# Retention q and k projections of an encoder trunk as four blocks of seven half-size products, with another order of the attention section and a planner that counts latencies between engines

## The chip, the cores and the metric

The kernel runs on one core of one Trainium2 chip. The metric is the device time of one execution in microseconds (us); a run of the comparison takes several executions, and their median is used. The profile comes from one further execution, recorded instruction by instruction. Engine names in it: PE is the matrix engine (PEld its weight loads), DVE the vector engine, ACT the scalar engine, POOL the GpSimd engine, SP the engine that issues plain DMAs.

## The reference, cut to what matters

Two encoder layers on 512 tokens of width 1024, in float32. Each layer has one wide input projection whose columns are split into the parts below; the change touches how `q_r` and `k_r` (512 columns each, four heads of 128) are computed.

```python
IN_SIZES = (NA_W, NA_W, NA_W, RET_QK_W, RET_QK_W, RET_V_W, RET_V_W, D_MODEL, D_MODEL)
...
    for i in range(DEPTH):
        proj = x @ w_in[i]
        q_na, k_na, v_na, q_r, k_r, v_r, g_r, gate_a, gate_b = jnp.split(proj, IN_SPLITS, axis=-1)
        ya = neighbourhood_attention(...)
        yb = bidirectional_retention(q_r.reshape(B, T, RET_HEADS, RET_QK_DIM),
                                     k_r.reshape(B, T, RET_HEADS, RET_QK_DIM),
                                     v_r, g_r, ret_decay_f[i], ret_decay_b[i])
        merged = jax.nn.sigmoid(gate_a) * (ya @ w_branch_a[i]) + jax.nn.sigmoid(gate_b) * (yb @ w_branch_b[i])
        y = merged @ w_out[i]
        x = layer_norm(DEEPNORM_ALPHA * x + y, ln1_g[i], ln1_b[i])
        ffn = conv_glu_ffn(x, w_up[i], conv_w[i], conv_b[i], w_down[i])
        ple = jax.nn.sigmoid(x @ w_ple_gate[i]) * (p[i] @ w_ple_proj[i])
        x = layer_norm(DEEPNORM_ALPHA * x + ffn + ple, ln2_g[i], ln2_b[i])
    return x
```

Retention rotates q and k (rotary embedding), forms decayed scores within a chunk and a decayed state across chunks, normalises each head and gates it.

## The kernel before

**Precision.** Every float32 operand of a product is split into a high and a low part (`split`: ACT casts `hi`, DVE subtracts to get `lo`), and `mm3` makes each product from three matmuls: hi by hi, hi by lo, lo by hi. A 512 KB chunk of weights thus costs one cast on ACT and one subtraction on DVE before PE can use it. Chunks marked "sent" (here those with numbers 20 to 23, among others) get `lo` from a second DMA that adds the weights onto the negated `hi`, so they cost no DVE instruction.

**Two ways to make a projection.** A plain tile (`gemm_t`) is 128 output columns by all 512 tokens: 8 pieces of the depth times 3 matmuls, 24 matmuls of 512 moving columns, into a PSUM bank named `gt`. A block is a two-by-two arrangement of tiles computed by seven half-size products (Strassen's scheme in Winograd's form), named a, c, t1, t2, d, t3 and t4; each is 24 matmuls of 256 moving columns (`product_t`, L1717) into banks named `u`, `v` and `w`. A block reads four weight chunks; the weights of t1, t2, t3 and t4 are sums of chunks, made in place by four accumulating DMAs from POOL. The sums of activations (`Sx`, tiles `sh` and `sl`) exist anyway. For a block of q and k tiles, `qk_block` (L1759) gathers the seven results into two SBUF tiles `uh` through `halves` (L1744), four times by a copy on ACT and three times by an addition on DVE, and hands the halves to the functions that follow a projection. In the kernel before, the three gate blocks 2, 3, 4 and the two blocks 5, 6 of attention q and k run this way; blocks 7 and 8 (retention q and k) are written in the code but not in the order, and retention q and k are the eight plain tiles `q0` to `q3` and `k0` to `k3` of a layer.

**The attention section** of a layer is the walk through the tuple `FILL` (L46): an entry such as `2t1` is product t1 of block 2, `R0` the next of four steps of retention head 0 (scores and the transposed k; state; output and group norm; transposition of the result into `ybt`), `N0` the next of three steps of attention head 0 (scores and softmax; transposition `pt`; output `na`), `vn` a piece of the attention values, `bb0` a tile of the retention branch's output projection, `xn` the load of the residual. After it come the merge (`mt`), the output projection, the first layer norm (`proj_ln`, `done1`, which transposes the normalised rows back with PE), and the gated MLP.

**The planner.** From the attention section to the last but one down-projection of a layer, the order of every engine's instructions is worked out when the program is built, by a list scheduler (`_order`, L466): it keeps a modelled time, a cost for each instruction (`_costs`), due times, counts of free buffers, and starts on each engine the first instruction in order of due time whose inputs are ready. PE keeps the written order, but in the attention section it may take any of the next `FILL_WIN` = 10 products. The due times are shaken by random numbers from the seeds in `SET`, one entry per layer, and `_best` repeats the pass up to 12 times with raised priority for what PE waited on. On the chip the engines run these fixed orders and wait for each other through semaphores.

A reader will meet these names: `lo`, `hi` the two parts of a weight chunk (`rawa`, `rawt`, `raw` the chunk itself), `t` and `kf` the rotated q and k, `qk` their split, `kz` the decayed k, `ta` and `a` the decayed scores, `yb` the normalised head, `qn`, `kn`, `kl` the attention q and k, `S` the attention scores, `xn` the residual rows, `x1t` the normalised activations.

```python
            def qk_block(b, kind):
                ps, first = bank_of(b, kind)
                product_t(kind, ps, first)
                st = keep.setdefault(b, {})
                i = halves(kind, st, ps)
                if i is not None:
                    h = st[i]
                    m = 2 * (b - 5 if b < 7 else b - 7) + 1 - i
                    for f, g in enumerate((na_q, na_k) if b < 7 else (q_head, k_head)):
                        g(m, h[:, f])
```

Of the kernel before, what the change touches and what calls it, by code (L numbers as in the profile page):

```python
# [42 lines left out]

FILL_WIN = 10
FILL_AT = (36, 40, 56, 24, 28, 8, 20)
FILL = (tuple('2a 3a 2c 3c q0 2t1 3t1 k0 2t2 3t2 2d 3d 4a 2t3 3t3 4c 2t4 4t1 k1 3t4 4t2 R0 4d q1 R0 4t3 R0 4t4 5a R0 R1 5c 5t1 k2 R1 q2 R1 5t2 5d R2 q3 R1 6a 6c R2 k3 R2 5t3 5t4 R3 6t1 6t2 R2 6d 6t3 R3 N0 N1 6t4 R3 vn N0 N1 vn R3 N2 vn N3 vn N0 N1 N2 bb0 N3 N4 bb1 N5 N6 bb2 N2 N4 N7 bb4 N3 N5 N6 bb5 N7 bb6 N4 bb7 N5 N6 xn N7 bb3'.split()),) * 2  # L46
ORD = ('vector', 'scalar', 'tensor', 'gpsimd', 'sync')
RESIDENT = {(l, c) for l in range(DEPTH) for c in range(68, 72)}

# [16 lines left out]

DOWN = ("a", "c", "t1", "t2", "d", "t3", "t4")
CAP = {"unit.u": 30, "xt.xt": 1, "raw.raw": 3, "wsplit.hi": 3, "wsplit.lo": 3, "tmp.t": 6, "bias.tb": 2, "bias.cw": 2, "bias.B": 2, "psum.b": 8}
COST = {"issue": 1.0, "send": 0.4, "load": 1.45, "add": 3.0, "land": 4.2}
EARLY = {"w": 14, "g": 13, "s": 15, "c": 13, "d": 13, "t3": 14, "a": 28, "t1": 38, "t2": 30, "t4": 18}  # L70
AHEAD, OVERLAP = 14, 0.08
_SET = dict(soon=5, hold=6, reserve=10, load=16, work=25, scale=1.0, spare=2, near=10, seed=0, shake=0.0)
SET = {1: dict(soon=3, hold=6, reserve=4, load=14, work=25, scale=1.0, spare=1, near=10, seed=651, shake=1), 2: dict(soon=3, hold=10, reserve=8, load=16, work=30, scale=1.0, spare=0, near=14, seed=903, shake=2)}
ROUNDS = 12


# [242 lines left out]
def _costs(o):  # L319
# [3 lines left out]
    if "dma" in o.name:  # L323
        o.dur = COST["issue"] if o.eng == "gpsimd" else COST["send"]
        ref = next((x for x in o.outs + o.ins if isinstance(x, Ref) and x.parts is not None), None)
        o.dma = (COST["add"] if o.k.get("accum_op") is not None else COST["load"]) * _size(ref) / 1024
        o.land = COST["land"]
    elif o.eng == "vector":
# [59 lines left out]
def _dues(jobs):  # L388

    soon = lambda j: SET[j.plan]["soon"] if j.plan else 5  # L390

# [74 lines left out]
def _order(jobs):  # L466
# [18 lines left out]
    for e in ENGINES:  # L485
# [6 lines left out]
        if e != "tensor":  # L492
            for p, s in segs:
                if p:
                    seed, amount = SET[p]["seed"], SET[p]["shake"]
                    rnd = random.Random(seed * 7 + len(e))
# [4 lines left out]
    free_at = {e: 0.0 for e in ENGINES}  # L501
    heap, t, pipe, order, lag, table = [0.0], 0.0, 0.0, [], 0.0, 0
    back, count, total, lost = [], 0, len(jobs), 0.0
    held = {}
    while count < total:
# [5 lines left out]
        for e in ENGINES:  # L511
# [66 lines left out]
            j = best  # L578
# [5 lines left out]
                x.pop(j, None)  # L584
            j.start = t
            j.done = t + dur
            free_at[e] = j.done - (OVERLAP if e in ("vector", "scalar") else 0.0)
            if j.dma:
                pipe = max(pipe, j.done) + j.dma
                j.done = pipe + j.land  # L590
# [1 line left out]
                b.pick = p  # L592
            for b in j.bufs:
                left[b] -= 1
                b.last = max(b.last, j.done)
                if not left[b]:
                    heapq.heappush(back, (b.last, id(b), b.options[b.pick]))
                    heapq.heappush(heap, b.last)
            for n in j.next:
                n.wait -= 1  # L600
                n.ready = max(n.ready, j.done)
            heapq.heappush(heap, j.done)
            heapq.heappush(heap, free_at[e])
            q.remove(j)
            order.append((j, picks))
# [61 lines left out]
def trunk(tc, wpack, x_nat, x_tr, head, p_tr, rpb, decay, ln_par, ln_col, conv, cos_t, sin_t, dist, xi_d, zd, mask, ident_d, out):  # L667
# [5 lines left out]
    with ExitStack() as es:  # L673
# [109 lines left out]
        def fill_items(l):  # L783
# [6 lines left out]
            out, vn = [], iter(plain_items(l, "vn"))  # L790
            for k in FILL[l]:
                if k == "vn":
# [500 lines left out]
        for l in range(DEPTH):  # L1293
# [537 lines left out]
            vns = na_v()  # L1831
            for f in FILL[l]:
                if f in heads:
# [629 lines left out]
def _pack(l, w_in, w_ba, w_bb, w_out, w_up, w_down, w_pg, w_pp):  # L2463
# [3 lines left out]
    def four(b, q, k, m):  # L2467
        if f"{b}a" not in FILL[l]:
            return [x for i in (m, m + 1) for x in (_stat(q)[i], _stat(k)[i])]
# [98 lines left out]
```

## Time and profile before

| what | value |
|---|---|
| time, median of 3 (lowest, highest) | 1669.72 us (1669.39, 1670.58) |
| the profiled execution: its time, its span | 1667.82 us, 1666.1 us |
| DVE, ACT, POOL busy in the span | 1265.7, 949.1, 258.8 us |
| attention section of layer 0, of layer 1 | about 109 to 379 us, 937 to 1206 us |
| last part (1600 to 1666 us): PE busy | 57.56 of 66 us |

The span is the time from the first to the last recorded instruction; the rest of the execution's time lies around it. The two sections were found by the tiles that PE works on (the first product of block 2, and the first tile of the merge). "Busy" counts an engine while any instruction of it runs, so matmuls, which overlap, keep PE busy without a break where the next one starts in time; what matters to the end is where PE is not busy, and how long the stream of matmuls itself is.

### The profile page before, as it was taken

The page shows a single profiled execution, that of the slowest core. Times are in us where ns is not written, and L with a number is a line of the kernel's source. Part 1 is how long each engine was busy: PE and PEld are TensorE (multiplying, and loading weights), DVE is VectorE, ACT ScalarE, POOL GpSimd, SP SyncE. Part 2 cuts the span into 40 slices and gives each one's busy share as a digit, 9 for nine tenths or more (in the row PEclk, how much of TensorE's full clock was granted, in tenths as well). Part 3 has the DMA queues.
Part 4 walks back from the last instruction along what each step waited for, and adds up shares of the span by engine and source line. Part 5 has one row for each costly group of instructions (what it writes and reads, how often), then busy time and mean ns, then how long its engine had stood idle before and what let it go on. Part 6 is the DMA issues. An engine that isn't in the chain of part 4 may idle for free.

```text
span 1666.1 us, 24182 instructions
## 1 busy us (share of the span) xinstructions
PE 1651.4 (99%) x9189; PEld 1443.2 (87%) x9189; DVE 1265.7 (76%) x1907; ACT 949.1 (57%) x1427; POOL 258.8 (16%) x312
## 2 busy tenths in 40 slices
PE   9999999999999999999999999999999999999997
PEld 7889999888788899898888899998888888988986
DVE  7756689976877858858876566899789687686788
ACT  6765446943456546446476645578534574563564
POOL 1111121210201111112012011222001011111113
PEclk9999999999999999999999999999999999999999
DMA  8988775775586888888678786758665878888884
GB/s 306 248 228 211 190 177 113 170 214 182 151 272 180 204 248 210 233 232 205 197 226 224 190 214 173 181 113 190 197 210 156 278 187 234 237 194 233 243 199 117
DMA packets 101365, 340.15 MB, mean 204 GB/s; under 512 B 11521, under 2 KB 16129, under 8 KB 101249
## 3 DMA queue, kind: packets, MB, share of 16 engines
q0 software_dynamic: 38736, 138.95, 42.8%
q1 hardware_dynamic: 62512, 199.66, 32.9%
q8 instruction: 72, 1.18, 0.3%
q14 instruction: 45, 0.36, 0.1%
HBM read 311.31 MB, written 25.69 MB: 202 GB/s over the span
## 4 chain that ended last, share of the span: by engine, by line
PE 69%; DVE 2%; issue 1%; POOL 0%; ACT 0%; DVEq 0%; POOLq 0%; ACTq 0%
PE gt L257 26%; PE u L257 19%; PE v L257 11%; PE w L257 5%; PE gn L257 3%; PE x L257 1%; PE o L257 1%; PE na L257 0%; PE pt L257 0%; PE tr L257 0%; PE ns L257 0%; PE s L257 0%; PE st L257 0%; DVE kl L257 0%; PE ybt L257 0%
## 5 line engine op out<-in xcount | busy, mean ns | idle before, releaser
L257 PE MATMUL gt<-x1t,hi 128*128 128x512 f32 x896 | 276.4, 390 | 0.0
L257 POOL DMA_DIRECT2D rawa<-in_wpack x126 | 113.5, 924 | 895.0 <-DVE lo L257 686.7
L257 DVE TENSOR_TENSOR lo<-rawa,hi 128x1024 fp32r<-128x1024 f32 (+1 forms) x166 | 196.9, 1194 | 70.5 <-ACT hi L257 70.0
L257 DVE TENSOR_TENSOR lo<-raw,hi 128x1024 fp32r<-128x1024 f32 x167 | 200.6, 1207 | 65.4 <-ACT hi L257 63.8
L257 ACT CAST hi<-rawa 128x1024 fp32r<-128x1024 f32 x166 | 169.1, 1028 | 105.7 <-DMA rawa<-in_wpack 54.7
L257 ACT CAST hi<-raw 128x1024 fp32r<-128x1024 f32 x167 | 171.7, 1038 | 63.0 <-PE v L257 12.5
L257 PEld LDWEIGHTS gt<-x1t,hi 128*128 128x128 f32 x896 | 166.7, 188 | 33.3
L257 PE MATMUL gt<-x1t,lo 128*128 128x512 f32 x448 | 174.3, 389 | 0.0
L257 PE MATMUL gt<-xt,hi 128*128 128x512 f32 x384 | 118.8, 390 | 0.0
L257 PEld LDWEIGHTS gt<-x1t,lo 128*128 128x128 f32 x448 | 84.1, 188 | 17.7
L257 PEld LDWEIGHTS gt<-xt,hi 128*128 128x128 f32 x384 | 71.0, 188 | 14.0
L257 PE MATMUL gn<-hi,mt 128*128 128x512 f32 x256 | 80.2, 391 | 0.0
L257 PE MATMUL gt<-ybt,hi 128*128 128x512 f32 x256 | 79.7, 393 | 0.0
L257 PE MATMUL gt<-xt,lo 128*128 128x512 f32 x192 | 74.7, 389 | 0.0
L257 POOL DMA_DIRECT2D lo<-in_wpack x48 | 42.4, 884 | 188.7 <-ACT lo L257 150.2
L257 PE MATMUL v<-hi,sh 128*128 128x512 f32 x184 | 71.6, 389 | 0.0
L257 PE MATMUL v<-lo,sh 128*128 128x512 f32 x184 | 71.6, 389 | 0.0
L257 PE MATMUL v<-hi,sl 128*128 128x512 f32 x184 | 71.6, 389 | 0.0
L257 PE MATMUL u<-hi,sh 128*128 128x512 f32 x168 | 65.4, 389 | 0.0
L257 PE MATMUL u<-lo,sh 128*128 128x512 f32 x168 | 65.4, 389 | 0.0
L257 PE MATMUL u<-hi,sl 128*128 128x512 f32 x168 | 65.3, 389 | 0.0
L257 DVE SCALAR_TENSOR_TENSOR gg<-gt,cw,gg 128x511 f32<-128x511 f32 x56 | 41.9, 747 | 26.5 <-ACT gg L257 25.9
(302 smaller groups left out, 4490.9 us busy)
## 6 DMA issues: line engine op xcount, KB each, us to landing
raw<-in_wpack SPq DMA_DIRECT2D x163, 512.0 KB, 5.8
rawa<-in_wpack POOLq DMA_DIRECT2D x120, 512.0 KB, 6.6
hi<-in_wpack POOLq DMA_DIRECT2D x48, 512.0 KB, 6.5
lo<-in_wpack POOLq DMA_DIRECT2D x48, 512.0 KB, 6.7
rawa<-in_wpack SPq DMA_DIRECT2D x40, 512.0 KB, 6.6
rawt<-in_wpack SPq DMA_DIRECT2D x40, 512.0 KB, 6.5
rawt<-in_wpack POOLq DMA_DIRECT2D x40, 512.0 KB, 9.0
sx<-s_scr SPq DMA_DIRECT2D x32, 512.0 KB, 8.3
```

Of the source, the lines that this page charges most:

```text
L257: r = o.call(*[real(x) for x in o.a], **{k: real(v) for k, v in o.k.items()})
```

## The change

`FILL` is another order, in which `7a` to `7t4` and `8a` to `8t4` stand in place of `q0` to `q3` and `k0` to `k3`; the function that packs the weights (`four`, L2467) makes block chunks of the same four chunks as soon as the names are in `FILL`. The seeds and shaken due times go (`SET` holds the defaults), and the scheduler gets other costs: issuing a DMA on POOL 0.88 instead of 1.0 us, an overlap of successive instructions of 0.083 us on DVE and 0.097 us on ACT, and a latency added after an instruction (`AFTER`) and before one that waits for another engine (`BEFORE`). Nothing else is edited; the sent chunks 20 to 23 are no longer sent, since only plain chunks can be.

```diff
--- before.py
+++ after.py
@@ -43,7 +43,7 @@
 
 FILL_WIN = 10
 FILL_AT = (36, 40, 56, 24, 28, 8, 20)
-FILL = (tuple('2a 3a 2c 3c q0 2t1 3t1 k0 2t2 3t2 2d 3d 4a 2t3 3t3 4c 2t4 4t1 k1 3t4 4t2 R0 4d q1 R0 4t3 R0 4t4 5a R0 R1 5c 5t1 k2 R1 q2 R1 5t2 5d R2 q3 R1 6a 6c R2 k3 R2 5t3 5t4 R3 6t1 6t2 R2 6d 6t3 R3 N0 N1 6t4 R3 vn N0 N1 vn R3 N2 vn N3 vn N0 N1 N2 bb0 N3 N4 bb1 N5 N6 bb2 N2 N4 N7 bb4 N3 N5 N6 bb5 N7 bb6 N4 bb7 N5 N6 xn N7 bb3'.split()),) * 2
+FILL = (tuple('2a 2c 7a 7c 2t1 7t1 7t2 2t2 7d 2d 2t3 7t3 7t4 3a 2t4 8a R0 8c R1 3c R0 3t1 8t1 R1 R0 R1 8t2 8d 8t3 R0 3t2 3d 8t4 3t3 4a R1 3t4 5a R2 4c 4t1 R2 5c R3 R3 5t1 4t2 R2 4d 5t2 R2 R3 5d R3 5t3 4t3 4t4 6a 6c 6t1 N0 N1 6t2 5t4 vn 6d N3 N0 N1 6t3 6t4 vn vn bb0 N2 vn N0 N2 N5 N1 bb2 N2 N3 N4 bb1 N6 N6 N6 N7 N5 N4 bb4 bb5 bb6 N7 N4 bb7 N5 N3 N7 xn bb3'.split()),)*2
 ORD = ('vector', 'scalar', 'tensor', 'gpsimd', 'sync')
 RESIDENT = {(l, c) for l in range(DEPTH) for c in range(68, 72)}
 
@@ -66,11 +66,14 @@
 
 DOWN = ("a", "c", "t1", "t2", "d", "t3", "t4")
 CAP = {"unit.u": 30, "xt.xt": 1, "raw.raw": 3, "wsplit.hi": 3, "wsplit.lo": 3, "tmp.t": 6, "bias.tb": 2, "bias.cw": 2, "bias.B": 2, "psum.b": 8}
-COST = {"issue": 1.0, "send": 0.4, "load": 1.45, "add": 3.0, "land": 4.2}
+COST = {"issue": 0.88, "send": 0.4, "load": 1.45, "add": 3.0, "land": 4.2}
 EARLY = {"w": 14, "g": 13, "s": 15, "c": 13, "d": 13, "t3": 14, "a": 28, "t1": 38, "t2": 30, "t4": 18}
-AHEAD, OVERLAP = 14, 0.08
+AHEAD = 14
+OVERLAP = {"vector": 0.083, "scalar": 0.097}
+AFTER = {"tensor": 0.2, "vector": 0.035, "scalar": 0.035, "gpsimd": 0.035}
+BEFORE = {"tensor": 0.11, "gpsimd": 0.05}
 _SET = dict(soon=5, hold=6, reserve=10, load=16, work=25, scale=1.0, spare=2, near=10, seed=0, shake=0.0)
-SET = {1: dict(soon=3, hold=6, reserve=4, load=14, work=25, scale=1.0, spare=1, near=10, seed=651, shake=1), 2: dict(soon=3, hold=10, reserve=8, load=16, work=30, scale=1.0, spare=0, near=14, seed=903, shake=2)}
+SET = {1: dict(_SET), 2: dict(_SET)}
 ROUNDS = 12
 
 
@@ -584,7 +587,7 @@
                 x.pop(j, None)
             j.start = t
             j.done = t + dur
-            free_at[e] = j.done - (OVERLAP if e in ("vector", "scalar") else 0.0)
+            free_at[e] = j.done - OVERLAP.get(e, 0.0)
             if j.dma:
                 pipe = max(pipe, j.done) + j.dma
                 j.done = pipe + j.land
@@ -592,14 +595,16 @@
                 b.pick = p
             for b in j.bufs:
                 left[b] -= 1
-                b.last = max(b.last, j.done)
+                b.last = max(b.last, j.done + AFTER.get(e, 0.0))
                 if not left[b]:
                     heapq.heappush(back, (b.last, id(b), b.options[b.pick]))
                     heapq.heappush(heap, b.last)
             for n in j.next:
                 n.wait -= 1
-                n.ready = max(n.ready, j.done)
+                n.ready = max(n.ready, j.done + (AFTER.get(e, 0.0) if n.eng != e or e != "tensor" else 0.0) + (BEFORE.get(n.eng, 0.0) if n.eng != e else 0.0))
             heapq.heappush(heap, j.done)
+            for n in j.next:
+                heapq.heappush(heap, n.ready)
             heapq.heappush(heap, free_at[e])
             q.remove(j)
             order.append((j, picks))
```

How instructions move, at three places. The first is DVE in the opening of layer 0's section, where the first retention q is rotated; before:

```order
L257 TENSOR_TENSOR lo_1215<-raw_1122,hi_1182 128x1024
L257 TENSOR_TENSOR t_198_1248<-gt_1185,sin_sb 64x512 x2
L257 TENSOR_TENSOR lo_1251<-rawa_947,hi_1246 128x1024
L257 TENSOR_TENSOR t_194_1253<-gt_1185,cos_sb 128x512
L257 TENSOR_TENSOR t_194_1253<-t_194_1253,t_198_1248 128x512
L257 TENSOR_TENSOR lo_1291<-rawa_929,hi_1286 128x1024
L257 TENSOR_TENSOR qk_1289<-t_194_1253,qk_1289 128x512
L257 TENSOR_SCALAR wx_1324<-dist_sb,nlg 128x384
L257 TENSOR_TENSOR lo_1327<-raw_1219,hi_1322 128x1024
```

and in the changed program:

```order
L260 TENSOR_TENSOR uh_1283<-uh_1283,v_1219 128x2x256
L260 TENSOR_TENSOR p_195_1246<-p_195_1246,u_1057 128x512
L260 TENSOR_TENSOR lo_1443<-rawa_1281,hi_1439 128x1024
L260 TENSOR_TENSOR lo_1447<-rawa_970,hi_1441 128x1024
L260 TENSOR_TENSOR uh_1283<-uh_1283,u_1123 128x2x256
L260 TENSOR_TENSOR t_219_1478<-uh_1283,sin_sb 64x512
L260 TENSOR_TENSOR t_218_1481<-uh_1283,cos_sb 128x512
L260 TENSOR_TENSOR t_219_1478<-uh_1283,sin_sb 64x512
L260 SCALAR_TENSOR_TENSOR kf_1508<-uh_1283,cos_sb 128x512
L260 TENSOR_TENSOR t_218_1481<-t_218_1481,t_219_1478 128x512
```

The rotation reads the PSUM bank `gt` before, and the gathered SBUF tile `uh` now; ahead of it stand additions into `uh`, and more subtractions `lo`.

The second is DVE where the first attention heads' scores `S` are read; before:

```order
L257 TENSOR_TENSOR ybt_2930<-ybt_2854,ybt_2930 128x512
L257 TENSOR_TENSOR ybt_2933<-ybt_2845,ybt_2933 128x512
L257 TENSOR_TENSOR uh_2830<-uh_2830,v_2740 128x2x256
L257 TENSOR_TENSOR kl_2958<-uh_2220,kn_2936 64x512 x4
L257 TENSOR_TENSOR su_2986<-st_2938,su_2986 128x512
L257 TENSOR_TENSOR uh_2830<-uh_2830,u_2509 128x2x256
L257 TENSOR_TENSOR S_3009<-ns_2996,B_2683 128x512
L257 TENSOR_TENSOR lo_3020<-rawa_2292,hi_2999 128x1024
L257 TENSOR_TENSOR S_3009<-ns_3004,B_2683 128x512
```

and in the changed program:

```order
L260 TENSOR_TENSOR ybt_3010<-ybt_2998,ybt_3010 128x512
L260 TENSOR_TENSOR ybt_3039<-ybt_3004,ybt_3039 128x512
L260 TENSOR_TENSOR qn_3041<-qs_2990,qn_3041 64x512
L260 TENSOR_TENSOR kl_3077<-uh_2662,kn_3044 64x512 x2
L260 TENSOR_TENSOR B_3082<-tb_1011,mask_sb 128x256 x2
L260 TENSOR_TENSOR lo_3086<-rawa_2802,hi_3079 128x1024
L260 TENSOR_TENSOR qn_3041<-qs_2990,qn_3041 64x512
L260 TENSOR_TENSOR kl_3077<-uh_2662,kn_3044 64x512 x2
L260 TENSOR_TENSOR uh_3075<-uh_3075,w_3090 128x2x256
L260 TENSOR_TENSOR S_3166<-ns_3154,B_2994 128x512
L260 TENSOR_TENSOR S_3166<-ns_3163,B_2994 128x512
```

Before, the last retention head's state `su` and the products of block 6 stand there; now the last retention head's `ybt` is done ahead of the attention heads' `qn` and `kl`.

The third is POOL at the end of layer 0's first layer norm, where `rstd` is the inverse deviation of a row tile; before:

```order
L257 DMA rawa_4340<-in_wpack 128x1024
L257 TENSOR_TENSOR rstd_4515<-ve_4507,mhalf 128x1
L257 TENSOR_TENSOR rstd_4561<-ve_4558,mhalf 128x1
L257 DMA rawa_4362<-in_wpack 128x1024
L257 TENSOR_TENSOR rstd_4655<-ve_4651,mhalf 128x1
L257 DMA rawa_4340<-in_wpack 128x1024
```

and in the changed program:

```order
L260 DMA rawa_4536<-in_wpack 128x1024
L260 TENSOR_TENSOR rstd_4714<-ve_4708,mhalf 128x1
L260 TENSOR_TENSOR rstd_4759<-ve_4756,mhalf 128x1
L260 TENSOR_TENSOR rstd_4846<-ve_4843,mhalf 128x1
L260 DMA rawa_4556<-in_wpack 128x1024
```

Before, one weight DMA is issued between the last two `rstd`; now it stands ahead of the third last, and the last three follow each other.

## The prediction, made before the changed kernel was run

> **What bounds the kernel now.** I read the page first, then the chain of waits, then busy time by stretch.
>
> ```profile
> span 1666.1 us, 24182 instructions
> PE 1651.4 (99%) x9189; PEld 1443.2 (87%) x9189; DVE 1265.7 (76%) x1907; ACT 949.1 (57%) x1427; POOL 258.8 (16%) x312
> ```
>
> PE is busy for 1651.4 of 1666.1 us, so the stream of matmuls sets the end: a change gains by a shorter stream or by closing the 14.7 us in which PE stands. The chain in order of time (start, length, what) shows what a product costs in that stream:
>
> ```profile
> 954.56 5.47 PE gt L257 x24
> ...
> 971.24 2.87 PE u L257 x24
> 974.12 2.88 PE v L257 x24
> 977.00 2.88 PE u L257 x24
> ```
>
> A plain tile takes 5.47 us for 24 matmuls of 512 columns (228 ns each), a half-size product 2.88 us for 24 of 256 (120 ns each); the next piece starts where one ends, so these are true costs. 120 is more than half of 228: seven for four saves 8% here, not an eighth.
>
> Where PE stands, by stretch (busy us and count of PE, PEld, DVE, ACT, POOL; granted clock; share of the DMA engines; GB/s). The first and third rows are the two attention sections:
>
> ```profile
> 109.00:379.00 270.00, 268.86 (x1806) 248.25 (x1807) 207.29 (x380) 165.81 (x299) 46.87 (x60) 1.00 0.71 176
> ...
> 590.00:710.00 120.00, 120.00 (x685) 106.02 (x684) 90.22 (x119) 63.55 (x80) 20.73 (x25) 1.00 0.87 226
> 937.00:1206.00 269.00, 267.85 (x1803) 247.31 (x1802) 207.47 (x380) 164.32 (x298) 46.85 (x60) 1.00 0.71 175
> 1008.40:1138.00 129.60, 128.48 (x923) 120.92 (x922) 110.87 (x222) 82.84 (x149) 27.77 (x37) 1.00 0.64 151
> ```
>
> PE stands for 1.14 us in the section of layer 0 and 1.15 in that of layer 1, 2.29 together. Nearly all of it is in the stretch where DVE is fullest; in layer 0:
>
> ```profile
> 230.00:290.00 60.00, 59.04 (x451) 56.86 (x450) 57.23 (x112) 38.14 (x66) 13.82 (x17) 1.00 0.64 152
> 290.00:310.00 20.00, 20.00 (x126) 17.71 (x125) 19.38 (x51) 18.64 (x43) 5.08 (x7) 1.00 0.60 137
> ```
>
> DVE is busy for 76.61 of 80 us (96%) and PE loses 0.96. The timeline names the place (start, length, engine, instruction):
>
> ```profile
> 281.75 1.29 DVE L257 TENSOR_TENSOR ybt<-ybt,ybt 128x512 fp32r<-128x512 f32 x2
> ...
> 283.56 2.80 DVE L257 TENSOR_TENSOR kl<-uh,kn 64x512 fp32r<-64x512 f32 x4
> ...
> 288.19 1.21 DVE L257 TENSOR_TENSOR lo<-rawa,hi 128x1024 fp32r<-128x1024 f32 x1
> ```
> ```profile
> 289.46 0.39 PE L257 MATMUL u<-xt,lo 128*128 128x256 f32 x1 [0.96 <-DVE lo L257]
> ```
>
> A weight's `lo` stands behind the last retention head and the first attention k, and PE waits 0.96 us for it.
>
> **The change part by part.** *The matmuls.* Each layer's eight plain tiles become two blocks. One block takes 7 x 2.88 = 20.16 us in place of 4 x 5.47 = 21.88; four blocks save 4 x 1.72 = **6.9 us** of PE's stream. The count agrees: 384 matmuls of 512 columns leave, 672 of 256 come.
>
> The Trainium skill, "TensorE: Matmul & The Clock Gate", section "Back-to-back issue gap", speaks against this: a sustained stream is put at about 131 ns per matmul at 512 columns and 81 ns at 128. A third of the way between them, an estimate from that page is 98 ns at 256, and the edit would cost 672 x 98 - 384 x 131 ns = 15.6 us. The rows above have 228 and 120 ns in this very stream; the measurement decides.
>
> *DVE and ACT.* Per layer there are 14 weight preparations for 8, and none of the 14 is sent where four of the eight were: 10 more `lo` on DVE, 10 more casts `hi` and 4 fewer ACT `lo` on ACT. Gathering adds 6 additions on DVE and 8 copies on ACT; 15 more table loads stand in ACT's new order, 7.5 a layer. Rows of layer 1's section (busy us, mean ns, idle before):
>
> ```profile
> L257 DVE TENSOR_TENSOR lo<-rawa,hi 128x1024 fp32r<-128x1024 f32 x19 | 23.2, 1219 | 8.8 <-ACT hi L257 8.7
> L257 DVE TENSOR_TENSOR uh<-uh,w 128x512 f32<-128x512 f32 x2 | 1.4, 684 | 0.1
> L257 ACT CAST hi<-rawa 128x1024 fp32r<-128x1024 f32 x19 | 19.9, 1047 | 26.2 <-PE gt L257 5.8 <-PE o L257 5.7 <-issue 5.1
> L257 ACT ACTIVATE lo<-hi 128x1024 fp32r<-128x1024 f32 x16 | 16.9, 1056 | 0.1
> L257 ACT ACTIVATE uh<-u 128x512 f32<-128x512 f32 x6 | 3.6, 592 | 5.3 <-PE u L257 4.5 <-DVE lo L257 0.7
> L257 ACT ACT_TABLE_LOAD x5 | 6.4, 1283 | 0.1
> ```
>
> DVE: 10 x 1.219 + 6 x 0.684 = 16.3 us more, 223.8 of the 265.6 us that are left (84%). ACT: 10 x 1.047 - 4 x 1.056 + 8 x 0.592 + 7.5 x 1.283 = 20.6 us more, 184.9 (70%). I cost ACT at nothing: PE's stream hides it, and its 80 free microseconds are the cover. If one table load in each section stood before a cast that PE waits for, that would be 1.28 us each, 2.6 together.
>
> A switch of tables is seen whole in layer 0's opening:
>
> ```profile
> 138.00 1.05 ACT L257 CAST hi<-raw 128x1024 fp32r<-128x1024 f32 x1
> 139.07 1.28 ACT L257 ACT_TABLE_LOAD   x1
> 140.36 0.91 ACT L257 ACTIVATE wx<-xi_sb,lgs 128x256 f32<-128x256 f32 x2
> ```
>
> From the cast's end to the next start it takes 1.31 us. The Trainium skill, "ScalarE: Activation LUTs", section "What ACT_TABLE_LOAD costs", adds a drain of about 1380 ns to a load of 1283 ns, 2.66 us in all; the load agrees, the drain does not show here. By the page ACT would have 10 us more a layer (73%), still covered.
>
> *Where PE stands in the section.* The retention heads move ahead of the attention heads, so the crowd at 288 us goes, and a new one comes earlier. Between the first score of `R0` and the last `ybt` of `R3` the new order has 816 matmuls of 256 and 48 of 128 columns, about 103 us, and 190 DVE instructions, of them 26 `lo` where 15 stood before. By rows like these
>
> ```profile
> L257 DVE SCALAR_TENSOR_TENSOR yb<-o,gmv,g 128x256 f32<-128x256 f32 x16 | 7.1, 476 | 0.0
> L257 DVE BATCH_NORM_STATS2 gn<-o 128x6 f32<-128x256 f32 x16 | 6.3, 420 | 2.3 <-PE o L257 2.3
> L257 DVE TENSOR_SCALAR yb<-yb,rstd 128x256 f32<-128x256 f32 x16 | 5.1, 349 | 0.2 <-POOL rstd L257 0.2
> L257 DVE SCALAR_TENSOR_TENSOR kz<-kz,zeta,kz 128x128 fp32r<-128x128 f32 x16 | 4.5, 342 | 0.5 <-ACT kz L257 0.4
> ```
>
> their durations sum to 26 x 1.22 + 68 of 512 elements x 0.687 + 16 x (0.476 + 0.420 + 0.349 + 0.342) + some 8 of small ones = 112 us. Neighbours overlap: the two `ybt` above last 1.29, not 1.37. The same sum for the old stretch, 1008.4 to 1138, is 123 us, where DVE was busy for 110.87: a factor of 0.90. So DVE has 101 us of work in 103, 97%, against 86% in that whole stretch before and 96% in the worst 80 us of it. Behind it the attention heads find DVE lighter than before. Bounds for PE's standing in both sections: none (-2.3 us), or the old rate of 0.96 in 80 us over both new crowds of 103 (2.5 us, +0.2). In the opening of the attention heads nothing of the old crowd is left, and the planner counts the latencies now, so I take the middle, **-1.0 us**.
>
> *The first layer norm.* Layer 0's last rows, before:
>
> ```profile
> 455.04 0.90 POOL L257 DMA_DIRECT2D rawa<-in_wpack  x1 [7.56 <-DVE ve L257]
> ...
> 455.65 1.87 POOL L257 TENSOR_TENSOR rstd<-ve,mhalf 128x1 f32<-128x1 f32 x1
> 455.91 1.22 DVE L257 TENSOR_TENSOR lo<-raw,hi 128x1024 fp32r<-128x1024 f32 x1
> ...
> 457.56 1.41 DVE L257 SCALAR_TENSOR_TENSOR xn<-xn,rstd,lnb 128x512 f32<-128x512 f32 x2 [0.43 <-POOL rstd L257]
> 458.37 1.38 PE L257 MATMUL tr<-ident,xn 128*128 128x128 f32 x8 [1.71 <-DVE xn L257]
> ```
>
> `rstd` stands behind a DMA issue and DVE waits 0.43 us for it. That issue now stands three instructions earlier; the `lo` ahead of `xn` stays. **-0.4 us**, bounds 0 and -0.43; in layer 1 the orders agree and nothing moves.
>
> *DMA.* Loads stay 16; accumulating transfers rise from 8 to 16 over both layers.
>
> ```profile
> q0 software_dynamic: 38736, 138.95, 42.8%
> q1 hardware_dynamic: 62512, 199.66, 32.9%
> ```
>
> A 0.524 MB transfer costs all 16 engines 0.329 x 1666.1 x 0.524 / 199.66 = 1.44 us on q1, and 2.69 on q0; with q0's 48 plain ones at 1.44, an accumulation costs 2.97. Four more a layer add 11.9 us to the 191 us that 0.71 of a section is: 0.76. I cost that at nothing: with 0.87 from 590 to 710 us PE missed nothing.
>
> Sum: -6.9 - 1.0 - 0.4 = **-8.3 us**, a span of 1657.8. The profiled execution took 1667.82 us, 1.9 less than the median of the runs, so the difference is put on the median: 1669.7 - 8.3 = **1661.4 us**.
>
> **The rivals.** *DVE gives the gain of the waits back.* If the new crowd makes several `lo` late, about 2.5 us a section are lost where 1.15 were, 2.7 more in all, with one table load a section in the way 2.6 more: 1669.7 - 6.9 - 0.4 + 5.3 = 1667.7 at most, 1665.8 in its middle. For it: 97%. Against it: 96% before cost one wait of 0.96.
>
> *Slower: weights come late in the opening.* Fifteen half-size products precede `R0`'s first step, with no plain tile between. Each block needs 4 x 1.44 + 4 x 2.97 = 17.6 us of DMA in 20.2 us of PE, 0.87, before anything else; that is 2.51 us a product.
>
> ```profile
> 110.00:160.00 50.00, 49.84 (x354) 46.89 (x353) 31.50 (x35) 29.59 (x38) 6.99 (x8) 1.00 0.81 195
> ```
>
> Here the opening's share is 0.81, of which nine products and two plain tiles in 37 us explain 9 x 2.51 + 2 x 1.44 = 25.5 us, 0.69; with the other 0.12 the new opening wants 0.99. It decides from a share of 1.0: were accumulations so slowed that the 43 us need 10% more, PE would wait 4.3 us, and the same again while blocks 3 and 8 are read, 17.2 in both layers: 1669.7 - 6.9 - 0.4 + 17.2 = 1679.6; one such wait a layer gives 1671.0. Against it: weights may be fetched ahead into 30 shared buffers, and the row of 0.87.
>
> *Half-size products are paced by their weight loads.* Each matmul has its own load of 128 columns:
>
> ```profile
> L257 PEld LDWEIGHTS gt<-x1t,hi 128*128 128x128 f32 x896 | 166.7, 188 | 33.3
> ```
>
> If a load's 188 ns set the pace, the edit would cost 672 x 188 - 384 x 228 ns = 38.8 us, 1708. Against it: 24 in 2.88 us, since loads overlap. By the page cited above it would be 1685, and the same rows are against it.
>
> *The change doesn't take hold*: the planner's new costs move only DVE and ACT, and new waits elsewhere eat the gain, about 1669.
>
> **How the numbers follow.** Forecast 0.72, with its own range of 1659 to 1664; DVE's crowd 0.13; late weights 0.10; no effect 0.04; paced by loads 0.01. Both bounds at their best give 1669.7 - 6.9 - 2.3 - 0.4 = 1660.1, and 1 us below that for the spread of runs is the low end. The high end, 1667, takes in most of the second case; late weights and the last two are left out, with little of the second. A measurement of this kernel tells 0.2%, 3.3 us, from no change: faster is under 1666.4. Faster: 0.72 + 0.08 = 0.80; same: 0.05 + 0.03 = 0.08; slower: 0.10 + 0.01 + 0.01 = 0.12.
>
> **What would show it.** Right: the chain has pieces of 2.88 us where 5.47 stood; PE's missing time in each section is near 0.6 us; DVE is near 97% between `R0` and `R3`; before layer 0's last transposes no `xn` waits for `rstd`; ACT's loads cause no wait of PE. Wrong: waits for `lo` between `R0` and `R3` (DVE's crowd), or for casts that wait for a DMA in the first 43 us of a section (late weights), or half-size products of other than 2.88 us.

## The result, and the profile after

| | median (lowest to highest) | ratio to the kernel before | 95% interval |
|---|---|---|---|
| before, same chip | 1669.56 us (1669.23 to 1670.58, 4 runs) | | |
| changed | 1660.07 us (1659.07 to 1660.66, 4 runs) | 0.9942 | 0.9924 to 0.9959 |
| changed, again on another chip | 1659.98 us (1659.64 to 1660.99, 5 runs) | 0.9952 | 0.9940 to 0.9965 |

The change makes the kernel faster by 9.5 us in the first comparison and 7.8 us in the second. The profiled execution of the changed kernel took 1660.66 us, 0.6 above its median, where that of the kernel before lay 1.9 below; so the spans differ by 7.3 us only, and the terms below are counted against these 7.3. The executions of the kernel before fall into two groups with none between 1668.7 and 1669.2 us: the four of the first comparison lie in the upper one, the profiled execution (1667.82) and the median of the second comparison (1667.74) in the lower. The page of the changed kernel (span; busy time and count by engine):

```profile
span 1658.8 us, 24840 instructions
PE 1645.4 (99%) x9477; PEld 1453.3 (88%) x9477; DVE 1289.4 (78%) x1939; ACT 986.4 (59%) x1470; POOL 263.9 (16%) x312
```

PE's busy time fell by 6.0 us, and the time in which PE stands from 14.7 to 13.4. Where it stands is read by stretch (length; busy time and count of PE, PEld, DVE, ACT, POOL; granted clock; share of the DMA engines; GB/s). First the end of each section up to the gated MLP in the kernel before:

```profile
379.00:470.00 91.00, 89.20 (x409) 73.78 (x408) 71.39 (x101) 40.59 (x65) 8.77 (x8) 1.00 0.55 171
...
1206.00:1290.00 84.00, 83.16 (x383) 68.72 (x382) 73.89 (x98) 36.30 (x59) 7.67 (x8) 1.00 0.60 185
```

and in the changed kernel the sections and these stretches, by layer:

```profile
109.00:376.50 267.50, 265.88 (x1955) 253.09 (x1954) 222.04 (x397) 183.93 (x319) 49.34 (x60) 1.00 0.77 188
376.50:466.00 89.50, 88.85 (x408) 73.33 (x406) 71.45 (x103) 42.05 (x67) 8.68 (x8) 1.00 0.54 166
...
933.00:1198.00 265.00, 264.22 (x1944) 251.47 (x1943) 219.39 (x394) 182.25 (x315) 49.67 (x60) 1.00 0.76 184
1198.00:1284.00 86.00, 85.31 (x394) 70.41 (x393) 76.25 (x103) 38.59 (x66) 9.60 (x8) 1.00 0.58 183
```

In the sections PE stands for 1.62 and 0.78 us, 2.40 together, where it was 2.29: nothing gained. At the layer norms it is 0.65 and 0.69, where it was 1.80 and 0.84: 1.30 gained. How the two share the gain differs between executions: in the profile of the changed kernel on the other chip (the second profile, span 1658.1 us), PE stands for 0.79 and 0.82 us in the sections and for 1.19 and 0.70 at the layer norms, so that 0.7 is gained in either. Who ends the waits, in the list of PE's waits (in total, times, longest, us), before:

```profile
PE tr L257 <- DVE xn L257: 2.5, 2, 1.7
PE u L257 <- DVE lo L257: 2.1, 3, 1.0
```

and after:

```profile
PE u L260 <- DVE p L260: 1.9, 2, 1.4
PE tr L260 <- DVE xn L260: 1.2, 3, 0.6
```

The waits for `lo` behind the old crowd are gone. A wait for `p` stands in their place, a tile of the part ahead of the section (values and gate of retention), and the timeline shows where it comes from:

```profile
104.60 1.28 ACT L260 ACT_TABLE_LOAD   x1 [2.12 <-DVE u L260]
105.89 1.15 ACT L260 ACTIVATE g<-u 128x512 f32<-128x512 f32 x2
106.95 1.98 ACT L260 CAST hi<-rawa 128x1024 fp32r<-128x1024 f32 x2
...
108.01 2.36 DVE L260 TENSOR_TENSOR lo<-rawa,hi 128x1024 fp32r<-128x1024 f32 x2 [2.90 <-ACT hi L260]
...
110.29 1.28 DVE L260 TENSOR_TENSOR p<-p,u 128x512 f32<-128x512 f32 x2
...
111.11 0.47 PE L260 MATMUL u<-hi,xt 128*128 128x512 f32 x1 [1.37 <-DVE p L260]
```

Read upwards: PE waits for the bank that the addition `p` frees; `p` stands behind two `lo`, these wait 2.90 us for casts `hi`, the casts stand behind the gate tile's Silu `g`, and that behind a load of its table, which itself waited 2.12 us for DVE. The order of ACT with its waits explains why a load waits; before:

```
L257 ACT_TABLE_LOAD
L257 ACTIVATE g_962<-u_158_921 128x512 [waits DVE]
```

and after:

```
L260 ACT_TABLE_LOAD [waits DVE]
L260 ACTIVATE g_962<-u_158_921 128x512 [waits Activation]
```

The tile `g` now takes a buffer that ACT itself used last, so its first instruction has two things to wait for, and the wait for DVE is put on the instruction ahead of it, the table load. Before, the load was over at 102.07 us, ahead of DVE's addition; now its 1.28 us come after the addition. The kernel before, at the same place:

```profile
100.79 1.28 ACT L257 ACT_TABLE_LOAD   x1
...
102.23 0.69 DVE L257 TENSOR_TENSOR u<-u,v 128x512 f32<-128x512 f32 x1
...
102.96 0.63 ACT L257 ACTIVATE g<-u 128x512 f32<-128x512 f32 x1 [0.89 <-DVE u L257]
```

### The profile page after: what moved, and what is told of

It reads as the page before. It is cut to its first block, busy times and chain, and to the rows that moved or that the text cites. A ratio compares the mean times of both kernels' runs of the same rounds, so it can differ in the third digit from the quotient of the medians.

```text
span 1658.8 us, 24840 instructions
## 1 busy us (share of the span) xinstructions
PE 1645.4 (99%) x9477; PEld 1453.3 (88%) x9477; DVE 1289.4 (78%) x1939; ACT 986.4 (59%) x1470; POOL 263.9 (16%) x312
## 4 chain that ended last, share of the span: by engine, by line
PE 94%; DVE 3%; issue 1%; ACT 1%; DMA 1%; POOL 0%; DVEq 0%; POOLq 0%; SPq 0%; ACTq 0%
PE gt L260 29%; PE u L260 27%; PE v L260 14%; PE gn L260 8%; PE w L260 7%; PE o L260 2%; PE x L260 1%; PE ns L260 1%; PE na L260 1%; PE pt L260 1%; DVE lo L260 1%; PE s L260 1%; PE tr L260 1%; DMA raw<-in_wpack 0%; DVE xn L260 0%
## 5 line engine op out<-in xcount | busy, mean ns | idle before, releaser
L260 POOL DMA_DIRECT2D rawa<-in_wpack x138 | 122.4, 908 | 945.0 <-DVE lo L260 719.2
L260 DVE TENSOR_TENSOR lo<-rawa,hi 128x1024 fp32r<-128x1024 f32 (+1 forms) x182 | 216.3, 1198 | 49.4 <-ACT hi L260 49.4
L260 ACT CAST hi<-rawa 128x1024 fp32r<-128x1024 f32 (+1 forms) x182 | 185.2, 1029 | 94.9 <-DMA rawa<-in_wpack 82.3
L260 PE MATMUL u<-xt,hi 128*128 128x256 f32 x448 | 81.8, 284 | 0.0
L260 PEld LDWEIGHTS u<-xt,hi 128*128 128x128 f32 x448 | 70.0, 192 | 0.2
L260 PE MATMUL u<-sh,hi 128*128 128x256 f32 x224 | 63.8, 285 | 0.0
```

Of the source, the lines that this page charges most:

```text
L260: r = o.call(*[real(x) for x in o.a], **{k: real(v) for k, v in o.k.items()})
```

## The experiments

### The planner alone, the old planner on the new order, plain tiles in the new order

*The planner alone*: the order and plain tiles of the kernel before, with the changed costs and settings.

```diff
-FILL = (tuple('2a 2c 7a 7c 2t1 7t1 7t2 2t2 7d 2d ...
+FILL = (tuple('2a 3a 2c 3c q0 2t1 3t1 k0 2t2 3t2 ...
```

> The planner's new costs and default settings, with the old order and its plain tiles. If the gain is the shorter stream of matmuls, this lies near the kernel before: 1669.6 us, between 1667 and 1672 by where PE's few waits fall, with PE busy near 1651 us. If it is the planner that gains (latencies counted, so fewer waits), it takes most of the 9.5 us: 1665 or less, with PE standing 10 us or less where it stood 14.7.

Measured: 1666.80 us, ratio 0.9989 (0.9980 to 0.9998); span 1664.7, PE busy 1652.1, standing 12.6. That is 0.2 us below the range that was expected if the stream makes the gain, and 1.8 above the one if the planner makes it: most of the gain is not the planner's. The planner alone closes 2.1 us of PE's waits, and the layer norms are among them: PE is busy 90.27 us in the stretch from 379 to 470, and 89.20 before.

*The old planner on the new order*: the blocks and the new order, the costs and seeds of the kernel before.

```diff
-FILL = (tuple('2a 3a 2c 3c q0 2t1 3t1 k0 2t2 3t2 ...
+FILL = (tuple('2a 2c 7a 7c 2t1 7t1 7t2 2t2 7d 2d ...
```

(against the kernel before)

> The new order with its four blocks, planned by the old costs and seeds. If the stream of matmuls makes the gain, 6.9 us stay: 1662.7 us, between 1660 and 1665, and the difference to the changed kernel is the waits of PE alone. If the planner makes it, this is at 1667 or above.

Measured: 1676.82 us, ratio 1.0054 (1.0041 to 1.0066), slower than the kernel before: a miss. The matmuls are the same 9477 as in the changed kernel, but PE stands for 23.1 us, 9.7 more, and is busy for 1651.5, 6.1 more. Part of the 6.1 is the clock (the last section); part is that a matmul of 256 columns with nothing behind it is recorded with 0.28 us where the next would start after 0.12, so that every break lengthens PE's busy time too. The crowds between `R0` and `R3` by stretch, first of the changed kernel, then of this one:

```profile
160.00:263.00 103.00, 102.75 (x858) 102.34 (x858) 99.01 (x194) 72.98 (x112) 21.68 (x25) 1.00 0.70 172
983.00:1087.00 104.00, 103.75 (x865) 103.13 (x864) 99.61 (x195) 73.48 (x112) 22.12 (x26) 1.00 0.69 173
```
```profile
160.00:263.00 103.00, 100.48 (x822) 98.48 (x821) 96.71 (x184) 69.74 (x107) 17.62 (x22) 1.00 0.68 167
983.00:1087.00 104.00, 98.42 (x789) 96.06 (x788) 94.46 (x167) 61.32 (x97) 15.86 (x18) 0.98 0.61 146
```

In the changed kernel DVE rests 4.0 and 4.4 us in its crowds, and PE loses 0.25 in each. Here DVE rests 6.3 and 9.5 us and PE loses 2.5 and 5.6: in these two rows, what DVE rests beyond 4 us comes out at PE nearly one for one. In the two runs of the next section it is less regular: DVE rests 4.4 and 7.4, 9.2 and 9.0 us, and PE loses 1.1 and 2.3, 4.3 and 4.5. The waits are spread over several links, for example:

```profile
PE s L257 <- ACT qk L257: 1.3, 1, 1.3
PE kz L257 <- DVE kf L257: 1.2, 1, 1.2
```

*Plain tiles in the new order*: everything of the change but the blocks.

```diff
-... 2a 2c 7a 7c 2t1 7t1 7t2 2t2 7d 2d 2t3 7t3 7t4 3a ...
+... 2a 2c q0 2t1 k0 2t2 2d 2t3 q1 k1 3a ...
```

> The new order and planner with plain tiles: q0, k0, q1, k1 stand where products c, t2, t3, t4 of block 7 stood, q2 to k3 likewise for block 8, and the other six products go. If the stream makes the gain, this is 4 x 1.72 = 6.9 us slower than the changed kernel: 1667.0 us, between 1665.5 and 1669, with PE busy near 1652 us. If the order of the section makes it, it is within 2 us of the changed kernel, 1660 to 1662.

Measured: 1671.23 us, ratio 1.0017 (1.0008 to 1.0026). Against the changed kernel's second profile (span 1658.1 us) its span of 1668.4 is 10.3 us longer: 1651.9 - 1644.8 = 7.1 us of busy PE, the stream, and 16.5 - 13.3 = 3.2 us of waits. So the new order is no gain by itself: with plain tiles it is worse than the old one, though DVE is busy only 80 us in the 103 of layer 0's crowd. The blocks' 7 us stands by itself. What the new order is worth to the blocks is not shown: no run has them in an order nearer to the old one.

### Which half of the planner: costs or seeds

*Old costs, default settings* (the new order, old costs, no seeds) and *old seeds* (the changed kernel with the seeds put back). "Seeds" stands for all of `SET`: the seeds, the shaken due times and the settings beside them go together, and which of them matters is not taken apart.

```diff
-SET = {1: dict(soon=3, ..., seed=651, shake=1), 2: dict(soon=3, ..., seed=903, shake=2)}
+SET = {1: dict(_SET), 2: dict(_SET)}
```

(against the run with the old planner; the second run has the reverse against the changed kernel)

> The new order with its four blocks, the planner's old costs (no latencies between engines, issue 1.0, overlap 0.08), but the default settings in place of the two seeds. If what made the run with the old planner slow is the seeds and shaken due times, which were drawn for the old order, most of the gain is back: within 4 us of the changed kernel, 1659 to 1664 us, with PE standing no more than 5 us between R0 and R3 of both layers. If it is the missing latencies, this is as slow as the run with the whole old planner: 1674 us or above.

> The other half: the changed kernel with its new costs, and the old seeds and settings put back. If the seeds are what hurts, 1670 us or above, with PE's waits between R0 and R3 back (8 us or more in both layers). If the latencies are what helps, within 4 us of the changed kernel: 1664 us or less.

Measured on the new order with its blocks:

| | old seeds | default settings |
|---|---|---|
| old costs | 1676.82 us, 1.0054 | 1669.30 us, 1.0007 (0.9998 to 1.0016) |
| new costs | 1677.16 us, 1.0055 (1.0041 to 1.0068) | 1660.07 us, 0.9942 |

The expectation that the seeds are the whole loss is half right. With the old seeds the new costs gain nothing; without them they gain 9 us. Dropping the seeds gains 7.5 us with the old costs and 17 with the new ones. Here both edits to the planner are needed to keep the blocks' 7 us. But each cell is one worked-out order, and the first run of the next section shows that one more instruction in each layer is enough to move the time by 3.7 us; no run tries other seeds, so how much of the 7.5, 9 and 17 us is the luck of single orders stays open.

### The table load that waits

*Silu early*: one small instruction ahead of the additions, so that the table is in place.

```diff
                     elif kind == "d":
                         product(kind, v[hp], False)
+                        if hp:
+                            nc.scalar.activation(pre, mhalf[:, :1], AF.Silu)
```

> The changed kernel with one added ACT instruction per layer, a Silu of a constant column (128x1) ahead of the additions whose results the gate tile's Silu reads, so that the load of its table has no wait to carry. In the changed kernel that load stands in the opening of each section with a wait on DVE of 2.1 to 2.4 us, and PE then waits 1.37 and 0.5 us for an addition p. If the load behind its wait causes PE's standing there, both waits go: 1658.2 us (1.9 less), and PE stands near 0.2 us in each opening. If DVE's load itself makes p late, nothing changes: 1660.1 us, and the wait for p stays above 1 us.

Measured: 1663.72 us, ratio 0.9972 (0.9961 to 0.9983), slower than the changed kernel: a miss by both theories. The opening is as expected (the stretch from 109 to 160 us has PE busy for 50.97 of 51 us, 49.63 and 50.47 in the two profiles of the changed kernel), but the planner, given one more instruction, worked out another order for layer 0, and PE stands 4.1 us in the crowd there:

```profile
160.00:263.00 103.00, 98.92 (x814) 97.32 (x813) 94.14 (x182) 66.28 (x105) 19.36 (x22) 1.00 0.69 166
```
```profile
L260 DVE SCALAR_TENSOR_TENSOR kz<-kz,zeta,kz 128x128 fp32r<-128x128 f32 x16 | 5.1, 347 | 5.8 <-ACT kz L260 5.7
```

(the second row is the group of `kz` on DVE in the same stretch: busy, mean ns, and the idle time before it; 1.6 us in the changed kernel). The timeline shows one such place: a table load and `wx` ahead of the `kz` on ACT that the next step waits for.

```profile
174.93 1.28 ACT L260 ACT_TABLE_LOAD   x1
...
176.64 0.51 ACT L260 ACTIVATE wx<-wx 128x384 f32<-128x384 f32 x1
177.06 0.61 ACT L260 ACTIVATE kz<-kz,zeta 128x128 fp32r<-128x128 f32 x2
177.70 0.35 DVE L260 SCALAR_TENSOR_TENSOR kz<-kz,zeta,kz 128x128 fp32r<-128x128 f32 x1 [2.08 <-ACT kz L260]
...
180.02 0.36 PE L260 MATMUL st<-vh,kz 128*128 128x256 f32 x1 [1.51 <-DVE kz L260]
```

*Silu early, the order kept*: the small instruction is put in when the order is already fixed. For this and for the runs below, an instruction can be attached to another one and is issued directly ahead of it:

```diff
+            if o.pre:
+                self.tc.keep_in_program_order(o.pre(real))
             r = o.call(*[real(x) for x in o.a], ...)
...
+                            if hp and not i:
+                                prog.add = lambda real: tc.nc.scalar.activation(real(pre), real(mhalf)[:, :1], AF.Silu)
                             g_tile(hp, i, t)
```

> The changed kernel itself, on the chip that the next three run on: 8 to 9.5 us faster than the kernel before. It is what they are compared with.

> As silu_early, but the small Silu is put in after the order has been worked out, directly ahead of the gate tile's Silu, so that every other instruction keeps the place it has in the changed kernel. If the load of the table behind its wait causes PE's standing in the openings (1.37 and 0.5 us for p), this is 1.9 us faster than the changed kernel, and the stretch between R0 and R3 keeps its 0.25 us of standing PE; the 4 us that silu_early lost there in layer 0 were then the re-planned order's. If the early Silu itself harms that stretch, the 4 us are lost here too: 2 us slower than the changed kernel.

Measured, on one chip: the changed kernel 1659.98 us, with the kept order and the early Silu **1658.31 us** (1657.97 to 1659.47), ratio to the kernel before 0.9943 (0.9929 to 0.9956); a gain of 1.7 us between ranges that do not touch, where 1.9 was expected. The waits for `p` are gone from PE's list (1.1 us in the changed kernel's profile on this chip), and the crowds keep their 0.25 us. So the load's share of the gain is 1.1 us by the profiles; another 0.6 of the difference between them is the wait for `xn` at the layer norm (1.7 to 1.1), where the same `rstd` lasts 2.65 us in one and 1.52 in the other, as it also does in two profiles without the early Silu (below). The opening now, where the load ends before DVE has added for `g`:

```profile
100.59 1.28 ACT L1427 ACT_TABLE_LOAD   x1
...
101.88 0.20 ACT L1427 ACTIVATE pre<-mhalf 128x1 f32<-128x1 f32 x1
...
102.95 0.63 ACT L264 ACTIVATE g<-u 128x512 f32<-128x512 f32 x1 [0.86 <-DVE u L264]
...
104.78 1.98 ACT L264 CAST hi<-rawa 128x1024 fp32r<-128x1024 f32 x2
105.85 2.36 DVE L264 TENSOR_TENSOR lo<-rawa,hi 128x1024 fp32r<-128x1024 f32 x2 [1.64 <-ACT hi L264]
```

This version is the fastest of all that ran, and faster than both kernels.

### How much room DVE has

Sixteen dead DVE instructions, put in at three places with the order kept.

```diff
+                    prog.add = lambda real: tc.nc.vector.tensor_reduce(real(dead), real(cos_sb), axis=AX.X, op=ALU.max)
                     nc.vector.tensor_mul(ta.rearrange(...), ...)
```

(in the crowd; for the attention heads it stands behind `nmx`, for the MLP ahead of the first eight additions to `R` of a layer)

> The changed kernel with 16 dead DVE instructions (a maximum over 512 columns of a constant, some 0.6 us each), put in after the order has been worked out, one ahead of each multiplication ta of the retention scores: 8 in each layer's crowd between R0 and R3, some 5 us, where DVE has 4.0 and 4.4 us free. If DVE's crowd is at its limit, what exceeds the free time shows in PE: 2 to 6 us slower than the changed kernel, with PE waiting for lo, kz, qk or qx in that stretch. If PE has cover left and only single waits matter, it is within 1 us of it.

> The control: the same 16 dead DVE instructions, one behind each attention head's scores instead, 8 in each layer, where DVE is busy some 75% of the time. If only the crowd between R0 and R3 is at its limit, this is within 0.5 us of the changed kernel. If any added DVE work in the section costs PE, it is as slow as the run with the same instructions in the crowd.

> The same 16 dead DVE instructions in a third place: 8 in each layer's gated MLP, ahead of additions to R (569 to 583 us in layer 0), where DVE is busy for 9.9 of 14 us and PE stands nowhere. If what counts is whether DVE has free time within a few microseconds of the place, this is within 0.6 us of the changed kernel, a ratio to the kernel before near 0.995, and no new wait of PE stands there. If any added DVE work between products costs PE, it is as slow as the two runs before it: a ratio near 0.997, 2.9 us above the changed kernel.

| 16 dead instructions of 0.676 us (10.8 in all) | median | PE stands (changed kernel on the chip of the first two: 13.3) |
|---|---|---|
| in the crowd | 1662.89 us, 0.9970 | 16.0 us |
| in the attention heads | 1662.86 us, 0.9970 | 15.5 us |
| in the MLP | 1661.32 us, 0.9955 (0.9941 to 0.9968) | 14.9 us |

In the crowd it came as forecast: 5.4 us more of DVE in 4.0 and 4.4 us of free time, and PE is busy 101.50 and 102.51 us where it was 102.75 and 103.75. But the control failed: the same work in the heads, where DVE was taken to be 75% busy, costs as much. The mean over that stretch hid pieces in which DVE is full: the new waits in them, for `lo` and `S`, make 1.5 of the 2.9 us, and the rest is not placed. Pieces of the changed kernel, the first two around dead instructions in the heads, the third and fourth around those in the MLP:

```profile
279.00:287.00 8.00, 8.00 (x60) 7.63 (x60) 8.00 (x12) 7.78 (x11) 1.72 (x2) 1.00 0.94 238
...
340.00:352.00 12.00, 12.00 (x70) 10.49 (x69) 11.94 (x32) 8.47 (x23) 2.28 (x3) 1.00 0.73 167
```
```profile
556.00:564.00 8.00, 8.00 (x37) 6.64 (x36) 8.00 (x13) 5.78 (x8) 1.71 (x2) 1.00 0.66 155
...
565.00:577.00 12.00, 12.00 (x54) 9.94 (x54) 9.12 (x13) 1.81 (x3) 1.74 (x2) 1.00 0.94 282
```

PE's new waits lie in the full pieces: at 285 and 350 us in the heads, at 561 us in the MLP (and at the same places of layer 1); at 561 us the first two of the MLP's eight stand. The other six, from 566 to 576 us, where DVE is busy 9.12 of 12, cost PE nothing. So the time of the third run fits neither expectation: it is 1.3 us above the changed kernel, and the waits for `k` behind the first two instructions of each layer are 1.2 of it. Together the three places say that the share of a section does not tell what added work costs, and that free time near the place does; "near" is some 10 us here, in pieces that were chosen after the waits were seen.

### How much room ACT has

Sixteen dead ACT instructions in the crowd, the order kept.

```diff
+                    prog.add = lambda real: tc.nc.scalar.copy(real(xi_sb), real(xi_sb))
                     split(a[:, 0, :], a[:, 1, :], ta)
```

> The changed kernel with 16 dead ACT instructions (a copy of a constant 128x512 onto itself, some 0.6 us each), put in after the order has been worked out, one ahead of each cast a in the crowd between R0 and R3: 8 in each layer, some 5 us, where ACT is busy 73.0 of 103 us. The prediction cost ACT's new work at nothing under the cover of its free time. If that holds, this is within 1 us of the changed kernel, a ratio near 0.995. If DVE has nothing to do when a cast is late, each late cast lengthens DVE's own 99 of 103 us: 2 to 5 us slower than the changed kernel, a ratio of 0.9965 to 0.9985, with DVE's idle time in the crowd above its 4 us, ended by ACT.

Measured: 1668.84 us, ratio 1.0001 (0.9992 to 1.0009): 9.9 us of dead work (16 x 0.620) take all that the change gave. The numbers are beyond both theories, and the cause is another. In each layer one wait holds nearly all of it:

```profile
PE o L264 <- ACT su L264: 4.7, 2, 3.0
```
```profile
181.91 0.58 ACT L264 COPY p<-v 128x512 f32<-128x512 f32 x1 [4.04 <-DMA gb_scr<-p]
182.40 0.62 ACT L264 CAST qx<-t 128x512 fp32r<-128x512 f32 x1
182.91 0.59 ACT L264 CAST su<-st 128x512 fp32r<-128x512 f32 x1
...
183.56 0.38 PE L264 MATMUL o<-su,qx 128*128 128x256 f32 x1 [3.02 <-ACT su L264]
```

With the added instructions the temporary tile `p` was given another buffer, one whose content a DMA to `gb_scr` was still saving; ACT waits 4.04 us for that DMA, with `qx` and `su` queued behind. So this run does not tell what 5 us of ACT's work cost by themselves, and that stays open. In the three runs with dead DVE instructions some tiles lie in other buffers too, but in layer 0 DVE's rows ahead of the new waits show no wait for a DMA; in the run with the kept order and the early Silu every tile keeps its buffer. What it shows is that a copy of 0.58 us at the head of ACT's queue, when it has to wait for a DMA, can hold PE for 3 us in this stretch.

## Why the prediction was right, by its steps

The forecast was 1661.4 us with 1659 to 1664 as its own range; 1660.07 is in it, and the kernel is faster, as forecast. The spans gained 7.3 us, and 8.0 by the second profile, of the 8.3 forecast. That the time came out below the forecast and not above it comes from the base: the 8.3 were taken from a median of 1669.7, while the terms had been read from the execution of 1667.82. Step by step:

- *The stream of matmuls, -6.9 us*: right. PE's busy time fell by 6.0 between the two profiles and by 6.6 in the two sections alone (268.86 + 267.85 to 265.88 + 264.22, with bounds that are rough to some tenths); the run with plain tiles in the new order has 7.1. The chain has half-size products of 2.88 us where plain tiles of 5.47 stood. Pacing by weight loads is out. In the chain of the changed kernel:

```profile
119.67 2.88 PE w L260 x24
```

- *PE's standing in the sections, -1.0*: wrong in the first profile, +0.1; in the second it is -0.7. The costs behind it held: DVE is busy for 222.0 and 219.4 us in the sections where 223.8 was worked out, ACT for 183.9 and 182.3 where it was 184.9. The part on DVE's crowd held too: 96% in both crowds (99.01 of 103, 99.61 of 104) where 97% was worked out, and 0.25 us of standing each. What failed is the step after it, "In the opening of the attention heads nothing of the old crowd is left ... so I take the middle": it looked for new waits only behind DVE's crowd, and the new ones stand in the opening of the section, ahead of that crowd: 1.37 us in layer 0 (0.53 in the second profile) and 0.53 in layer 1.
- *ACT's work, 0*: wrong in the openings, by the case that the prediction priced and set aside: a table load before a cast that PE waits for. It was priced at 2.6 us for both layers; the waits that it causes are 1.9 and 1.1 us in the two profiles, and the run that takes it away gains 1.7. ACT's free 80 us a section are no cover: the run with the re-planned Silu lost 4 us in a crowd in which ACT was busy 66 of 103 us.
- *The first layer norm, -0.4*: right in direction, too small: -1.3 in the first profile (1.15 in layer 0, 0.15 in layer 1), -0.75 in the second. `rstd` no longer stands behind a DMA issue. In the first profile it lasts 1.52 us, and `xn` does not wait for it; PE waits 0.55 us at the transposes where it waited 1.71.

```profile
451.79 1.52 POOL L260 TENSOR_TENSOR rstd<-ve,mhalf 128x1 f32<-128x1 f32 x1 [6.87 <-DVE ve L260]
...
453.96 1.41 DVE L260 SCALAR_TENSOR_TENSOR xn<-xn,rstd,lnb 128x512 f32<-128x512 f32 x2
...
454.76 1.38 PE L260 MATMUL tr<-ident,xn 128*128 128x128 f32 x8 [0.55 <-DVE xn L260]
```

In the second profile the same `rstd` lasts 2.65 us, `xn` waits for it again, and PE waits 1.09 us:

```profile
450.53 2.65 POOL L260 TENSOR_TENSOR rstd<-ve,mhalf 128x1 f32<-128x1 f32 x1 [6.88 <-DVE ve L260]
...
453.22 1.42 DVE L260 SCALAR_TENSOR_TENSOR xn<-xn,rstd,lnb 128x512 f32<-128x512 f32 x2 [0.44 <-POOL rstd L260]
...
454.03 1.38 PE L260 MATMUL tr<-ident,xn 128*128 128x128 f32 x8 [1.09 <-DVE xn L260]
```

The planner alone has this gain too (PE waits 0.64 us there). The term was sized by the 0.43 us that DVE waited, but with `rstd` earlier the `lo` and `xn` behind it moved as well; by how much each is not taken apart. The prediction's sign that no `xn` waits for `rstd` held in one execution and failed in the other.

- *DMA, 0*: right. The sections' share is 0.77 and 0.76 where 0.76 was worked out, and no cast that waited for a DMA held PE in the first 43 us; late weights are out.

Summed, the waits gained 1.3 us, and 1.4 in the second profile, close to the forecast 1.4. In the first profile 1.1 too little in the sections and 0.9 too much at the layer norms cancel, in the second 0.3 and 0.35. That the end came out right is partly luck.

*The rivals.* That DVE gives the waits back did not happen in the changed kernel, but it was nearer than a chance of 0.13 says: with the old seeds, the old costs or one more instruction the same blocks lose 4 to 17 us, and with the old planner they cost more than its 1667.7 us at most (1676.8). With this order it is the planner's two edits together that keep the crowd closed.

## What to carry to other kernels

A shorter stream on the bounding engine is only worth its full count if the engines that feed it keep pace, and these may be tuned to the old order: settings and seeds chosen for one order should be dropped or chosen anew when the order changes. Judge the room of a feeding engine in pieces of some 10 us, by what stands behind the instruction that is to be added, not by the share over a section. Where a change of order adds switches of ACT's tables, look at which of them have a wait on the load itself, and put a small activation of the next kind ahead of the data.

## What the runs showed of the hardware

A short stop of PE can cost more than its length. In the run with dead ACT instructions, PE stands for 3.02 us from 180.5 us and for another 0.46 before 184.4; then its granted clock falls (by stretch, the clock is the third number from the end):

```profile
180.00:184.00 4.00, 0.92 (x6) 0.51 (x4) 0.95 (x2) 2.09 (x5) 0.00 (x0) 1.00 0.35 135
184.00:187.00 3.00, 2.60 (x16) 2.61 (x17) 2.50 (x4) 3.00 (x7) 0.00 (x0) 0.75 0.00 0
187.00:190.00 3.00, 3.00 (x20) 3.00 (x20) 2.66 (x7) 1.24 (x4) 0.00 (x0) 0.68 0.00 0
```

Matmuls of 256 columns start every 0.21 us from 185.45 to 188.81 us instead of every 0.120: 16 starts, some 1.4 us lost, an estimate from these rows. From 190 to 195 us the clock is 1.00 again. The same follows waits of 1.65 and 0.46 us in layer 1 (clock 0.59 from 1011 to 1014 us), and in the run with the old planner a row of waits of 0.63 to 1.27 us between 994 and 1004 us (0.62 from 1006 to 1010). The Trainium skill, "TensorE: Matmul & The Clock Gate", section "What's actually happening", puts the fall of the clock after an idle window of about 3.4 us; here 3.02 and 0.46 us were enough, and so were shorter pieces close together. Neither profile of the changed kernel, nor that of the kernel before, has such a fall in or between its sections, with single waits of 1.1 to 1.7 us. Yet a wait of that length can be followed by one: in the run with the old costs and default settings PE waits 1.65 us ahead of the eight transposes of layer 0's first layer norm, where the kernel before waited 1.71, and the clock is 0.62 from 457 to 461 us. What decides between the two is not shown.

A load of ACT's tables can carry a wait of the activation behind it, as in the openings of the changed kernel (2.12 and 2.37 us for DVE); it then costs its 1.28 us after the data came, not before.

The same POOL instruction on 128x1 can last 1.52 us in one execution and 2.65 in another: `rstd` at layer 0's first layer norm, by the two profiles of the changed kernel, with 6.9 us of idle POOL ahead of it in both. The run with dead DVE instructions in the attention heads and that with plain tiles in the new order have 2.66 us at this place. Why stays open; it is worth half a microsecond of PE's time here.
